# Gate applied where the heads' outputs leave PSUM, and a last norm summed on the tensor engine, in a two-layer hybrid trunk

## The chip, the core and the metric

The kernel runs on one core of a Trainium2 chip. The metric is the device time of one execution in microseconds (us). A core has engines that each run their own instructions in order: TensorE (PE; its weight loads are listed apart as PEld), VectorE (DVE), ScalarE (ACT), GpSimd (POOL) and SyncE (SP, which here only issues DMA transfers). SBUF is the on-chip memory that all engines read and write, PSUM the memory that PE writes its sums to, DRAM the large memory outside, reached by DMA.

## The reference

x is 1024 tokens of 1024 channels. Layer 1 mixes tokens with a diagonal state-space model (S5), layer 2 with a chunked gated DeltaNet of 12 heads of 128 channels; both add a 4-head cross attention into 256 memory tokens. What matters here is how layer 2 ends:

```python
h = rmsnorm(x, norm_w[i])
qkv, a, b, gate_mix, q_x, gate_x = jnp.split(h @ gdn_w_in[j], [...], axis=-1)
o = gated_delta_chunked(q, k, v, g, beta)            # 12 heads of 128
y_mix = rmsnorm(o, norm_w) * silu(gate_mix)          # 1536 channels
y_x = cross_attn(q_x, mem_h, w_mem_kv[i]) * silu(gate_x)    # 512 channels
x = x + concatenate([y_mix, y_x]) @ w_out[i]
return rmsnorm(x, final_norm_w)
```

## The kernel before

Everything is float32. A large product is made of three PE matmuls (`mm3`, L107): each operand is split into a high part, rounded to a short mantissa, and the rest (`split`, L84: the high part is a cast on ACT, L86, the rest a subtraction on DVE, L73). Weights come through a ring of two tiles each (`weight`, L114): `wraw` by DMA on ACT's queue, `whi` cast on ACT, `wlo` subtracted on DVE. Small helpers record most instructions, so their lines recur: `dma` L70 (SP's queue), `tt` L73, `ts` L77 and L79, `stt` L82, `mm` L48 and `transpose` L51 for PE. A tile scheduler, not the code's lines, sets the order on each engine, from the program's order and priorities; the engines keep to it. PSUM has four buffers `pp` for the large products and four `ps_a` for the rest.

Layer 2's DeltaNet runs over 8 chunks of 128 tokens, in two units of 6 heads each: `g_step` makes a unit's outputs `o` (with the products `r`, `vd`, `vn` and the state `S`), `g_norm` (L1242) normalises them, turns them with PE transposes into channels by tokens in `ps_a`, copies them on ACT with the norm's weight `gnw` into `oT` (L1264), and writes `oT` to DRAM (`oTd`). The gates, silu already applied, lie in DRAM as 12 tiles of 128 channels by 1024 tokens (`gate2`). `attention` makes one head's output `po` for 512 tokens, multiplies it by its gate tile `sg` into `yx` and writes `yx` to DRAM (`yT`, `yT2`).

The output projection of layer 2 runs in two halves of 512 tokens; the first half holds the tokens of chunks 0 to 3, the second those of 4 to 7. `out2_inputs(half)` makes the 16 input tiles of a half: four from the attention, then 12 from the heads. For a head's tile it loads `zr` from `oTd` and `zg` from the gate, multiplies them on POOL, and splits the product into `oh` and `ol`. `zr` and `zg` have three buffers in the first half and five in the second. `out2` then makes 8 output columns; each takes two weight tiles and 16 input tiles, adds the residual `xr` into `xo` and its squares, `sq`, to the sum `facc`. The first half's tiles are made beside the last attention heads and chunk steps (about 1648 to 1698 us), its columns beside the steps and norms of the last chunks (1698 to 1798), and the second half's tiles beside the first half's last columns (1798 to 1836).

The last column (`last_column`) is cut into two blocks of 256 tokens, so that the first block's norm runs beside the second block's products. The norm sums the 128 channels on PE into token columns (`rstd_cols`), takes the inverse root by three iterations on DVE (`rsqrt`, with names ending in e, t and h, and a sign turned at the end by a multiplication by −1), spreads it over the partitions with PE (`on_partitions`) and scales 8 columns (`out_scale`): columns 2 and 5 by ACT and POOL, the other six by one DVE instruction each.

Of the kernel before, what the change touches and what calls it, by code (L numbers as in the profile page):

```python
# [11 lines left out]
F32 = mybir.dt.float32  # L12
F32R = mybir.dt.float32r
I32 = mybir.dt.int32
AF = mybir.ActivationFunctionType
ALU = mybir.AluOpType
# [37 lines left out]
class Kern:  # L54
# [135 lines left out]
        self.ts(var, ss[:, 0:nt], 1.0 / nch, MUL, EPS, ADD)  # L190
        return self.rsqrt(wp, var, (128, nt), name)

    def on_partitions(self, wp, cols, name):

        out = []
        nt = cols.shape[1]
        for t0 in range(0, nt, 4):
            n = min(4, nt - t0)
            rb = self.pa.tile([128, 512], F32, name="ps_a", tag="ps_a")
            for t in range(n):  # L200
                dg = self.tl(wp, (128, 128), name + "dg", bufs=2)
                self.ts(dg, self.ident, cols[:, t0 + t:t0 + t + 1], MUL)
                self.pe.matmul(rb[:, 128 * t:128 * t + 128], lhsT=self.ones, rhs=dg, start=True, stop=True)
            out.append(rb[:, 0:128 * n])
        return out

    def rows_to(self, dst, halves):
        o = 0
# [71 lines left out]
    def attention(self, layer, h, half, ap, dst):  # L280
        scale = 128 ** -0.5
        hs = slice(512 * half, 512 * half + 512)
        kv = []
        for o in (0, 4):
            raw = self.tl(ap, (128, 256), f"kvr{o}")
            self.dma(raw, self.kvd[layer][o + h])
            kv.append([self.tl(ap, (128, 256), f"kv{o}{i}", F32R) for i in "hl"])
            self.split(raw, *kv[-1])
        (kh, kl), (vh, vl) = kv
        q, sg = self.tl(ap, (128, 512), "q"), self.tl(ap, (128, 512), "sg")  # L290
        self.dma(q, self.qx[h][:, hs])
        self.dma(sg, self.gx[h][:, hs])
        qh, ql = self.tl(ap, (128, 512), "qh", F32R), self.tl(ap, (128, 512), "ql", F32R)
        self.split(q, qh, ql)
        pr = self.tl(ap, (128, 4, 256), "pr")
        mx, sm = self.tl(ap, (128, 4), "mx"), self.tl(ap, (128, 4), "sm")
        for t2 in range(2):
            sc = self.pa.tile([128, 2, 256], F32, name="ps_a", tag="ps_a")
            for j in range(2):
                t = 2 * t2 + j  # L300
                s = slice(128 * t, 128 * t + 128)
                self.mm3(sc[:, j], (qh[:, s], ql[:, s]), (kh, kl), True, True)
            m = mx[:, 2 * t2:2 * t2 + 2]
            self.v.tensor_reduce(out=m, in_=sc, axis=AX, op=ALU.max)
            self.ts(m, m, -scale, MUL)
            for j in range(2):
                t = 2 * t2 + j
                self.act.activation(pr[:, t], sc[:, j], AF.Exp, bias=mx[:, t:t + 1], scale=scale,
                                    accum_out=sm[:, t:t + 1])
        self.v.reciprocal(out=sm, in_=sm)  # L310
        for t in range(4):
            self.ts(pr[:, t], pr[:, t], sm[:, t:t + 1], MUL)
        yield
        ph, pl = self.tl(ap, (128, 2, 512), "ph", F32R), self.tl(ap, (128, 2, 512), "pl", F32R)
        for b in range(2):
            pt = self.pa.tile([128, 512], F32, name="ps_a", tag="ps_a")
            for t in range(4):
                self.pe.transpose(pt[:, 128 * t:128 * t + 128], pr[:, t, 128 * b:128 * b + 128], self.ident)
            self.act.copy(ph[:, b], pt)
            self.tt(pl[:, b], pt, ph[:, b].bitcast(F32), SUB)  # L320
        po = self.pa.tile([128, 512], F32, name="ps_a", tag="ps_a")
        for b in range(2):
            d = slice(128 * b, 128 * b + 128)
            self.mm3(po, (vh[:, d], vl[:, d]), (ph[:, b], pl[:, b]), b == 0, b == 1)
        yx = self.tl(ap, (128, 512), "yx")
        self.tt(yx, po, sg, MUL)
        self.dma(dst[:, hs], yx)
        yield


# [911 lines left out]
    def g_norm(self, c, hf, o, gp):  # L1242

        act, pe, tt, ts = self.act, self.pe, self.tt, self.ts
        cs = slice(128 * c, 128 * c + 128)
        ss = self.tl(gp, (128, 6), "oss")
        for h in range(6):
            sq = self.tl(gp, (128, 128), "osq")
            act.activation(sq, o[:, h], AF.Square, accum_out=ss[:, h:h + 1])
        rq = self.rq[:, c, 3 * hf:3 * hf + 3].unsqueeze(2).broadcast_to([128, 3, 2])  # L1250
        s2 = ss.rearrange("p (j e) -> p j e", e=2)
        tt(s2, s2, rq, MUL)
        tt(s2, s2, rq, MUL)
        ts(ss, ss, 1.0 / 128, MUL, EPS, ADD)
        y = self.rsqrt(gp, ss, (128, 6), "on")
        y2 = y.rearrange("p (j e) -> p j e", e=2)
        tt(y2, y2, rq, MUL)
        tt(o, o, y.unsqueeze(2).broadcast_to([128, 6, 128]), MUL)
        oT = self.tl(gp, (128, 6, 128), "oT")
        for h0, n in ((0, 4), (4, 2)):  # L1260
            ps = self.pa.tile([128, 4, 128], F32, name="ps_a", tag="ps_a")
            for h in range(n):
                pe.transpose(ps[:, h], o[:, h0 + h], self.ident)
            act.activation(oT[:, h0:h0 + n], ps[:, 0:n], AF.Copy, scale=self.gnw)  # L1264
        self.dma(self.oT[6 * hf:6 * hf + 6, :, cs].rearrange("t p k -> p t k"), oT)


    def out2_inputs(self, half, yp, *pools):
        hs = slice(512 * half, 512 * half + 512)
        y = self.half_tiles(yp, 512, lambda i: 1)  # L1270
        for i, k in enumerate([12, 13, 14, 15] + list(range(12))):
            wp, n = pools[i % 5 // 3 if len(pools) > 1 else 0]
            t = self.tl(wp, (128, 512), "zr", bufs=n)
            if k >= 12:
                self.dma(t, self.yT2[k - 12, :, hs])
            else:
                g = self.tl(wp, (128, 512), "zg", bufs=n)
                self.dma(t, self.oT[k, :, hs])
                self.dma(g, self.gate2[k][:, hs])
                self.tt(t, t, g, MUL, self.pool)  # L1280
            self.split(t, y[i][0], y[i][1])
        return y

    def out2(self, half, y, wp):
        n = 512
        hs = slice(n * half, n * half + n)
        acc = self.tl(wp, (128, n), "facc")
        xo = []
        for ct in range(KD):
            w = self.A["w_out"][1, ct]  # L1290
            pieces = w[:, 0:8], w[:, 8:16]
            x = self.tl(wp, (128, n), "xr", bufs=2)
            k = slice(n // TAU * half, n // TAU * (half + 1))
            self.dma(x.rearrange("p (t k) -> p t k", t=TAU),
                     self.x1[ct].rearrange("p (t k) -> p t k", t=TAU)[:, :, k])
            xo.append(self.tl(wp, (128, n), f"xo{ct}"))

            def add(p, s):
                xs = x.rearrange("p (t k) -> p k t", t=TAU)[:, s.start // TAU:s.stop // TAU]
                self.tt(xo[ct][:, s].rearrange("p (k t) -> p k t", t=TAU), xs,  # L1300
                        p.rearrange("p (k t) -> p k t", t=TAU), ADD)
                self.square_sum(wp, acc[:, s], xo[ct][:, s], ct == 0)

            if half == 1 and ct == KD - 1:
                self.last_column(wp, pieces, y, add, xo, acc)
            else:
                add(self.project(pieces, y)[0], slice(0, n))
            yield
        if half == 0:
            s = slice(0, n)  # L1310
            rb, = self.on_partitions(wp, self.rstd_cols(wp, acc, 1024, "fn"), "fn")
            self.out_scale(wp, xo, rb, half, s)
            yield

    def last_column(self, wp, pieces, y, add, xo, acc):
# [14 lines left out]
        col = self.rstd_cols(wp, acc[:, blocks[0]], 1024, "fn")  # L1330
        products(1, 1)
        rb = self.on_partitions(wp, col, "fn")[0]
        add(ps[1], blocks[1])
        col = self.rstd_cols(wp, acc[:, blocks[1]], 1024, "fn")
        self.out_scale(wp, xo, rb, 1, blocks[0])
        self.out_scale(wp, xo, self.on_partitions(wp, col, "fn")[0], 1, blocks[1])

    def out_scale(self, wp, xo, rb, half, s):
        o = slice(512 * half + s.start, 512 * half + s.stop)
        n = s.stop - s.start  # L1340
        r = self.tl(wp, (128, n), "fr")
        self.act.copy(r, rb)
        for k in range(KD):
            if k % 3 == 2:
                self.act.activation(xo[k][:, s], xo[k][:, s], AF.Copy, scale=self.fnw[:, k:k + 1])
                self.tt(xo[k][:, s], xo[k][:, s], r, MUL, self.pool)
            else:
# [84 lines left out]
    def build(self):  # L1432
        tc = self.tc
        with ExitStack() as st:
# [6 lines left out]
            self.ud, self.gy = D("ud", 12, (TAU, 128, 128)), D("gy", 12, (TAU, 128, 128))  # L1441
            self.gate = D("gate", 12)
            self.yT = dr.tile([16, 128, L], F32, name="yT")
            self.x1, self.gate2 = D("x1", 8), D("gate2", 12)
            self.yT2 = dr.tile([4, 128, L], F32, name="yT2")
            self.qkvd = dr.tile([24, 128, L], F32, name="qkv")
            self.qkv = [self.qkvd[i] for i in range(24)]
# [94 lines left out]
```

## Time and profile before

| | us |
|---|---|
| median of 3 runs | 1940.75 |
| lowest and highest | 1936.44, 1943.25 |
| the profiled execution | 1942.68 |
| its span, first to last instruction | 1940.6 |

The profile is of one execution. Its lines name a line of the kernel, the engine, the operation, what it writes and reads (`out<-in`), shapes, counts, the busy time and the mean of one in ns, and the idle time of the engine before it with the work that ended it. The granted clock is that of PE, 1.0 being full speed; its mean over the span is 0.987. A line of a helper, L73 above all, stands for many places, so groups are told apart by the tiles' names.

### The profile page before, as it was taken

Reading aid. Unit: us, or ns where it says so; the run is one execution under the profiler, and the core shown is the slowest. Engines: PE = TensorE matmul, PEld = TensorE weight load, DVE = VectorE, ACT = ScalarE, POOL = GpSimd, SP = SyncE. Lnnn points to the kernel's source line nnn. Section 1 sums busy time; section 2 is a strip of 40 time slices with the busy share of each in tenths; the row PEclk is TensorE's granted clock in tenths of the full one; section 3 lists DMA queues with packets and bytes.
Section 4 is the critical chain, followed back from the end, with each engine's and each line's share of the span. In section 5 each row is a group of like instructions: output and inputs, shape, how many; then the busy total and the mean of one; then the engine's idle time right before and its main releaser. Section 6 shows DMA issues by size and latency. Waiting matters only on the chain.

```text
span 1940.6 us, 28754 instructions
## 1 busy us (share of the span) xinstructions
PE 1858.6 (96%) x10386; PEld 1527.3 (79%) x10386; DVE 1288.0 (66%) x2484; ACT 963.2 (50%) x2057; POOL 132.3 (7%) x87
## 2 busy tenths in 40 slices
PE   6899999999989998999999989999999999799897
PEld 6788888788878886888778878878777888688686
DVE  7888898896564422664556645888734876787644
ACT  5345688786454412443343456664434654555321
POOL 3000000000202231000000000000000000300400
PEclk9999999999999999999999999999999999999998
DMA  7445555655844343654312478776446656874752
GB/s 236 142 138 136 165 170 159 169 158 144 262 153 146 120 160 103 218 159 141 109 67 93 134 218 239 214 211 190 134 123 226 206 168 196 257 233 135 227 155 87
DMA packets 254397, 325.17 MB, mean 168 GB/s; under 512 B 80816, under 2 KB 176624, under 8 KB 254256
## 3 DMA queue, kind: packets, MB, share of 16 engines
q1 hardware_dynamic: 228912, 238.40, 39.7%
q10 hardware_dynamic: 25344, 84.95, 14.9%
q8 instruction: 82, 1.34, 0.3%
q14 instruction: 59, 0.48, 0.1%
HBM read 213.20 MB, written 93.95 MB: 158 GB/s over the span
## 4 chain that ended last, share of the span: by engine, by line
PE 75%; DVE 8%; DMA 8%; ACT 4%; issue 3%; SPq 1%; POOL 0%; DVEq 0%; ACTq 0%; POOLq 0%
PE pp L48 59%; PE ps_a L48 12%; PE ps_a L51 3%; DMA yr<-gy 2%; DVE wlo L73 1%; SPq L70 1%; DMA kv<-kvt 1%; DMA E<-Grow 1%; DMA zr<-yT 1%; DMA zr<-oTd 1%; DVE ol L73 0%; POOL zr L73 0%; ACT whi L86 0%; DMA kq<-qkv 0%; DMA x<-in_xT_dram 0%
## 5 line engine op out<-in xcount | busy, mean ns | idle before, releaser
L48 PE MATMUL pp<-hh,whi 128*128 128x512 f32 x1216 | 495.2, 408 | 0.0
L48 PE MATMUL pp<-hl,whi 128*128 128x512 f32 x1216 | 478.7, 394 | 3.7 <-DVE hl L82 3.7
L48 PE MATMUL pp<-hh,wlo 128*128 128x512 f32 x1216 | 478.0, 393 | 0.0
L86 ACT CAST whi<-wraw 128x1024 fp32r<-128x1024 f32 (+1 forms) x180 | 183.2, 1019 | 373.5 <-PE pp L48 351.8
L73 DVE TENSOR_TENSOR wlo<-wraw,whi 128x1024 fp32r<-128x1024 f32 (+2 forms) x180 | 218.0, 1211 | 101.5 <-ACT whi L86 100.9
L48 PEld LDWEIGHTS pp<-hh,whi 128*128 128x128 f32 x1216 | 229.7, 189 | 50.6 <-issue 5.3
L48 PEld LDWEIGHTS pp<-hh,wlo 128*128 128x128 f32 x1216 | 229.5, 189 | 48.4
L48 PEld LDWEIGHTS pp<-hl,whi 128*128 128x128 f32 x1216 | 229.8, 189 | 47.0 <-DVE hl L82 4.8
L48 PE MATMUL pp<-oh,whi 128*128 128x512 f32 (+1 forms) x528 | 208.3, 395 | 10.7 <-ACT oh L86 6.7
L48 PE MATMUL pp<-oh,wlo 128*128 128x512 f32 (+1 forms) x528 | 209.5, 397 | 3.0 <-DVE wlo L73 3.0
L48 PE MATMUL pp<-ol,whi 128*128 128x512 f32 (+1 forms) x528 | 208.8, 396 | 1.3 <-DVE ol L73 1.3
L48 PEld LDWEIGHTS pp<-oh,whi 128*128 128x128 f32 x528 | 100.6, 191 | 33.5 <-ACT oh L86 8.1
L48 PEld LDWEIGHTS pp<-ol,whi 128*128 128x128 f32 x528 | 100.7, 191 | 26.5 <-DVE ol L73 3.8
L48 PEld LDWEIGHTS pp<-oh,wlo 128*128 128x128 f32 x528 | 100.8, 191 | 24.7 <-DVE wlo L73 4.3
L48 PE MATMUL pp<-yl,whi 128*128 128x512 f32 x288 | 114.2, 396 | 0.5 <-DVE yl L73 0.5
L48 PE MATMUL pp<-yh,wlo 128*128 128x512 f32 x288 | 114.0, 396 | 0.0
L48 PE MATMUL pp<-yh,whi 128*128 128x512 f32 x288 | 113.5, 394 | 0.0
L73 DVE TENSOR_TENSOR pj<-pp,hr 128x512 f32<-128x512 f32 x104 | 69.0, 685 | 53.1 <-PE pp L48 53.1
L82 DVE SCALAR_TENSOR_TENSOR pj<-cx,conv_w,pj 128x1024 f32<-128x1024 f32 x72 | 92.3, 1282 | 1.4
L73 DVE TENSOR_TENSOR cx<-pp,hr 128x512 f32<-128x512 f32 x48 | 32.4, 689 | 91.0 <-PE pp L48 91.0
L73 POOL TENSOR_TENSOR ye<-yh,yl 128x1024 f32<-128x1024 f32 x12 | 29.7, 2475 | 620.3 <-DVE yl L73 444.9
L73 POOL TENSOR_TENSOR zr<-zr,zg 128x512 f32<-128x512 f32 x24 | 38.0, 1604 | 444.9 <-DMA kq<-qkv 308.9
(352 smaller groups left out, 3173.7 us busy)
## 6 DMA issues: line engine op xcount, KB each, us to landing
wraw<-in_w_out_dram ACTq DMA_DIRECT2D x64, 512.0 KB, 3.9
wraw<-in_g_w_in_dram ACTq DMA_DIRECT2D x44, 512.0 KB, 4.0
wraw<-in_s_w_in_dram ACTq DMA_DIRECT2D x32, 512.0 KB, 4.0
R<-E SPq DMA_DIRECT2D x48, 256.0 KB, 3.9
gate<-pj SPq DMA_DIRECT2D x24, 512.0 KB, 4.3
qkv<-pj SPq DMA_DIRECT2D x24, 512.0 KB, 2.6
kq<-qkv SPq DMA_DIRECT2D x60, 192.0 KB, 4.1
wraw<-in_w_glu_dram ACTq DMA_DIRECT2D x24, 384.0 KB, 3.6
```

Of the source, the lines that this page charges most:

```text
L48: return self.pin(self.eng.matmul(*a, **kw))
L51: return self.pin(self.eng.transpose(*a, **kw))
L70: self.nc.sync.dma_start(out=out, in_=in_)
L73: (eng or self.v).tensor_tensor(out=out, in0=a, in1=b, op=op)
L82: self.v.scalar_tensor_tensor(out=out, in0=a, scalar=s, in1=b, op0=op0, op1=op1)
L86: self.act.copy(hi, src)
```

## The change

1. `g_norm` of chunks 4 to 7 loads the unit's gate (`og`, 128 x 6 x 128, one buffer) and multiplies by norm weight and gate in one DVE instruction per PSUM tile, in place of ACT's copy. `gate2` becomes one DRAM tensor, so that one DMA reaches six heads.
2. `out2_inputs` of the second half loads no gate and multiplies nothing. In the first half the product moves from POOL to DVE.
3. `attention` multiplies in place into `sg`; the tile `yx` is gone.
4. The last block's norm (`negative_rstd`) adds `facc` and the last squares in PSUM, runs each iteration on single columns with one dependent step less, and leaves its result negative; the sign goes into `on_partitions`. It is recorded at high priority. In the first block of the last column, ACT and POOL scale columns 1, 3, 5 and 7 instead of 2 and 5.

```diff
-    def on_partitions(self, wp, cols, name):
+    def on_partitions(self, wp, cols, name, sign=None):
...
-                self.ts(dg, self.ident, cols[:, t0 + t:t0 + t + 1], MUL)
+                self.ts(dg, self.ident, cols[:, t0 + t:t0 + t + 1], MUL, sign, sign and MUL)
...
+    def negative_rstd(self, wp, parts, nch, name):
+        n = parts[0].shape[1] // 128
+        ss = self.pa.tile([128, 512], F32, name="ps_a", tag="ps_a")
+        for t in range(n):
+            for i, p in enumerate(parts):
+                self.pe.matmul(ss[:, t:t + 1], lhsT=p[:, 128 * t:128 * t + 128], rhs=self.ones[:, 0:1],
+                               start=i == 0, stop=i == len(parts) - 1)
+        x, h, t = (self.tl(wp, (128, n), name + c) for c in "vht")
+        e = self.tl(wp, (128, n), name + "e", I32)
+        y = e.bitcast(F32)
+        self.ts(x, ss[:, 0:n], 1.0 / nch, MUL, EPS, ADD)
+        self.ts(e, x.bitcast(I32), 1, ALU.logical_shift_right)
+        self.ts(h, x, 0.5, MUL)
+        self.ts(e, e, -1.0, MUL, 1597463007.0, ADD)
+        for _ in range(3):
+            for j in range(n):
+                c = slice(j, j + 1)
+                self.stt(t[:, c], y[:, c], y[:, c], h[:, c], MUL, MUL)
+            self.stt(y, t, 1.5, y, SUB, MUL)
+        return y
...
-        yx = self.tl(ap, (128, 512), "yx")
-        self.tt(yx, po, sg, MUL)
-        self.dma(dst[:, hs], yx)
+        self.tt(sg, po, sg, MUL)
+        self.dma(dst[:, hs], sg)
...
         oT = self.tl(gp, (128, 6, 128), "oT")
+        if c >= 4:
+            g = self.tl(gp, (128, 6, 128), "og", bufs=1)
+            self.dma(g, self.gate2[6 * hf:6 * hf + 6, :, cs].rearrange("t p k -> p t k"))
...
-            act.activation(oT[:, h0:h0 + n], ps[:, 0:n], AF.Copy, scale=self.gnw)
+            if c < 4:
+                act.activation(oT[:, h0:h0 + n], ps[:, 0:n], AF.Copy, scale=self.gnw)
+            else:
+                self.stt(oT[:, h0:h0 + n], ps[:, 0:n], self.gnw, g[:, h0:h0 + n], MUL, MUL)
...
+            elif half:
+                self.dma(t, self.oT[k, :, hs])
             else:
                 g = self.tl(wp, (128, 512), "zg", bufs=n)
                 self.dma(t, self.oT[k, :, hs])
                 self.dma(g, self.gate2[k][:, hs])
-                self.tt(t, t, g, MUL, self.pool)
+                self.tt(t, t, g, MUL)
...
-            def add(p, s):
+            def add(p, s, total=True):
...
-                self.square_sum(wp, acc[:, s], xo[ct][:, s], ct == 0)
+                if total:
+                    self.square_sum(wp, acc[:, s], xo[ct][:, s], ct == 0)
+                    return
+                sq = self.tl(wp, p.shape, "sq", bufs=2)
+                self.act.activation(sq, xo[ct][:, s], AF.Square)
+                return sq
...
-        add(ps[1], blocks[1])
-        col = self.rstd_cols(wp, acc[:, blocks[1]], 1024, "fn")
-        self.out_scale(wp, xo, rb, 1, blocks[0])
-        self.out_scale(wp, xo, self.on_partitions(wp, col, "fn")[0], 1, blocks[1])
+        sq = add(ps[1], blocks[1], False)
+        with self.tc.high_priority(offset=200):
+            col = self.negative_rstd(wp, (acc[:, blocks[1]], sq), 1024, "fz")
+            last = self.on_partitions(wp, col, "fn", -1.0)[0]
+        self.out_scale(wp, xo, rb, 1, blocks[0], (1, 3, 5, 7))
+        self.out_scale(wp, xo, last, 1, blocks[1])
...
-    def out_scale(self, wp, xo, rb, half, s):
+    def out_scale(self, wp, xo, rb, half, s, beside=(2, 5)):
...
-            if k % 3 == 2:
+            if k in beside:
...
-            self.x1, self.gate2 = D("x1", 8), D("gate2", 12)
+            self.x1 = D("x1", 8)
+            self.gate2 = dr.tile([12, 128, L], F32, name="gate2")
```

On DVE, where the first half's tiles are made (about 1670 us), before; a row is a line, an operation, what it writes and reads, and a shape, and `ol` is the rest of a tile's split:

```order
L73 TENSOR_TENSOR ol_15198<-zr,oh_15197 128x512
L77 TENSOR_SCALAR pr<-pr,sm 128x256 x4
L82 SCALAR_TENSOR_TENSOR r<-ps_a,nbr_9715,r 128x128 x2
L73 TENSOR_TENSOR ol_15200<-zr,oh_15199 128x512
L73 TENSOR_TENSOR ol_15202<-zr,oh_15201 128x512
L82 SCALAR_TENSOR_TENSOR r<-ps_a,nbr_9715,r 128x128 x3
L73 TENSOR_TENSOR vd<-ps_a,dlr_9716 128x512
```

The same place of the change:

```order
L73 TENSOR_TENSOR ol_15179<-zr,oh_15178 128x512
L73 TENSOR_TENSOR zr<-zr,zg 128x512
L77 TENSOR_SCALAR mx<-mx 128x2
L73 TENSOR_TENSOR r<-ps_a,gbe_8478 128x512
L73 TENSOR_TENSOR r<-ps_a,gbe_8478 128x256
L73 TENSOR_TENSOR ol_15181<-zr,oh_15180 128x512
L332 RECIPROCAL sm<-sm 128x4
L82 SCALAR_TENSOR_TENSOR r<-ps_a,nbr_9696,r 128x128
L73 TENSOR_TENSOR zr<-zr,zg 128x512 x2
```

The products `zr<-zr,zg` now stand on DVE between the chunk step's `r` and the attention's `mx`.

On ACT, where the second half's tiles are made (about 1798 to 1830 us), before; `oh` is the cast of a tile, `whi` that of a weight tile, and `whi_17043` and `whi_17081` belong to the last columns of the first half:

```order
L86 CAST oh3_16814<-zr_16852 128x512
L86 CAST whi_17043<-wraw_17042 128x1024
L86 CAST oh4_16816<-zr_16856 128x512
L86 CAST oh5_16818<-zr_16863 128x512
L86 CAST oh6_16820<-zr_16870 128x512
L123 DMA wraw_17110<-in_w_out_dram 128x1024
L86 CAST oh7_16822<-zr_16877 128x512
L86 CAST oh8_16824<-zr_16884 128x512
L179 ACTIVATE sq_17005<-xo5_16942 128x512
L86 CAST whi_17081<-wraw_17080 128x1024
```

The same place of the change:

```order
L86 CAST oh2_16801<-zr_16837 128x512
L86 CAST whi_17034<-wraw_17033 128x1024
L86 CAST oh3_16803<-zr_16841 128x512
L86 CAST oh4_16805<-zr_16845 128x512
L86 CAST oh5_16807<-zr_16849 128x512
L123 DMA wraw_17102<-in_w_out_dram 128x1024
L86 CAST oh6_16809<-zr_16853 128x512
L86 CAST oh7_16811<-zr_16857 128x512
L86 CAST whi_17064<-wraw_17063 128x1024
```

Five casts of tiles stand between two casts of weights in both; the weight casts now come one tile earlier, and the tiles wait for a load alone.

On SP's queue, where the last chunks' outputs are written (about 1760 to 1800 us), before:

```order
L70 DMA oTd<-oT 128x6x128
L70 DMA xr<-x_99 128x8x64
L70 DMA oTd<-oT 128x6x128
L70 DMA xr<-x_100 128x8x64
L70 DMA oTd<-oT 128x6x128 x2
L70 DMA zr<-yT_114 128x512
```

The same place of the change:

```order
L70 DMA oTd<-oT 128x6x128
L70 DMA og<-gate_102 128x6x128
L70 DMA oTd<-oT 128x6x128
L70 DMA og<-gate_102 128x6x128
L70 DMA xr<-x_100 128x8x64
L70 DMA oTd<-oT 128x6x128
L70 DMA og<-gate_102 128x6x128
L70 DMA oTd<-oT 128x6x128
L70 DMA xr<-x_101 128x8x64
L70 DMA zr<-yT_103 128x512
```

Each unit's gate load stands behind the write of the unit before, and `og` has one buffer.

## The prediction

> **What bounds the kernel now.** I read the page's busy times first, then the last 300 us by stage: in each row the stretch, its length, the busy time of PE, PEld, DVE, ACT and POOL (instructions in brackets), the granted clock, the DMA share and GB/s.
>
> ```profile
> PE 1858.6 (96%) x10386; PEld 1527.3 (79%) x10386; DVE 1288.0 (66%) x2484; ACT 963.2 (50%) x2057; POOL 132.3 (7%) x87
> ...
> 1648.00:1698.00 50.00, 40.28 (x200) 31.06 (x199) 40.00 (x95) 25.91 (x75) 17.51 (x12) 0.97 0.82 258
> 1698.00:1798.00 100.00, 99.37 (x562) 84.48 (x561) 80.51 (x253) 53.76 (x175) 0.00 (x0) 1.00 0.64 187
> 1798.00:1836.00 38.00, 30.96 (x124) 24.27 (x123) 30.92 (x27) 15.28 (x23) 20.48 (x12) 0.91 0.75 236
> 1836.00:1925.00 89.00, 89.00 (x437) 73.78 (x436) 38.33 (x67) 21.74 (x27) 2.55 (x2) 1.00 0.41 121
> 1925.00:1941.00 16.00, 3.22 (x18) 2.47 (x17) 9.02 (x34) 1.06 (x3) 3.00 (x4) 0.62 0.40 132
> ```
>
> PE is the bound with 96% of the span, and the change removes no product. So only PE's holes count, and the end, where PE has nothing left. Between 1698 and 1798 PE is full (99.37 of 100), and between 1836 and 1925 wholly so. The holes are 9.7 us in 1648–1698, where the first half's 16 tiles are made beside the chunk steps ("stage 1"), 7.0 us in 1798–1836, where the second half's are made ("stage 2"), and the tail from 1925. Apart from six instructions behind 1836, which belong to the final scaling, POOL works in these two stages alone: 12 gate products each, 1.46 us apiece in stage 1 and 1.71 in stage 2. The changed order of instructions departs from the old one only from about 1650 us on, apart from the gate loads of layer 1's attention, so the rest keeps its time.
>
> **Stage 2: the second half's tiles lose load and product.** The waits of PE, then of ACT, in 1800–1835 (us in total, times, longest), and the matmuls after PE's second stall (start, us):
>
> ```profile
> PE pp L48 <- ACT whi L86: 4.0, 1, 4.0
> PE pp L48 <- DVE wlo L73: 3.0, 2, 1.7
> ...
> ACT oh L86 <- POOL zr L73: 10.5, 9, 3.1
> ...
> 1819.62 0.63 PE L48 MATMUL pp<-oh,whi 128*128 128x512 f32 x1
> ...
> 1822.61 0.56 PE L48 MATMUL pp<-ol,whi 128*128 128x512 f32 x1
> ...
> 1823.23 0.40 PE L48 MATMUL pp<-oh,whi 128*128 128x512 f32 x1
> ...
> 1824.85 0.39 PE L48 MATMUL pp<-ol,whi 128*128 128x512 f32 x1
> ```
>
> PE waits for weights, not for tiles: `whi` is cast on ACT, and ACT runs its instructions in order; the casts of the second half's tiles stand ahead of `whi` and wait 10.5 us for POOL's products. So the products hold the weights of the last columns of the first half. PE then restarts slowly: seven steps of 0.43 us from 1819.62 to 1822.61, against 0.23 from 1823.23 to 1824.85 (seven again). Eight of them cost 8 x 0.20 = 1.6 us. Without the POOL products a tile needs a cast on ACT and a subtraction on DVE:
>
> ```profile
> L73 DVE TENSOR_TENSOR ol<-zr,oh 128x512 fp32r<-128x512 f32 x13 | 16.9, 1316 | 6.3 <-ACT oh L86 5.8
> ...
> L73 DVE TENSOR_TENSOR ol<-zr,oh x32: 676/692/1774, 1647.2 to 1830.7; 128x512 fp32r<-128x512 f32 x32
> ```
>
> The first row is stage 2 alone, the second all 32 (shortest, median, longest). Beside POOL the subtraction took 1.32 us; the shortest is 0.68. Twelve tiles at 0.69 are 8.3 us, where POOL needed 20.5. What can go is 7.0 + 1.6 = **8.6 us**. Late next is the tile chain itself: last transposes, write to DRAM, read, cast. The changed order puts about 9 us of PE's own products ahead of those last transposes, so less stands behind them to cover the chain; with the first casts waiting for the write, a short stall can stay. I take −8, with −8.6 and −4 (half of the stall left) as ends.
>
> **Stage 1: the product moves from POOL to DVE.** PE's largest waits in 1636–1700, the subtraction's row there, and two rows of the queue that issues the loads:
>
> ```profile
> PE ps_a L48 <- ACT ph L319: 2.9, 1, 2.9
> PE ps_a L48 <- ACT vn L1214: 2.8, 2, 2.1
> ...
> PE pp L48 <- ACT oh L86: 1.3, 1, 1.3
> PE pp L48 <- DVE ol L73: 1.3, 3, 0.7
> ...
> L73 DVE TENSOR_TENSOR ol<-zr,oh 128x512 fp32r<-128x512 f32 x16 | 13.2, 842 | 9.0 <-ACT oh L86 8.8
> ...
> 1656.70 0.33 SPq L70 DMA_DIRECT2D zg<-gate  x1
> 1657.14 2.50 SPq L70 DMA_DIRECT2D zr<-oTd  x3
> ```
>
> Only 2.6 us of the 9.7 are waits for tiles; `ph` and `vn` belong to the attention and the chunk steps, which share ACT and DVE with the tiles. A 128x512 product with both inputs in SBUF and no POOL beside it is priced by the subtraction, 0.69; 12 of them add 8.3 us to DVE, busy 40.0 of 50, and the subtractions give back 16 x (0.842 − 0.692) = 2.4. Net 5.9 of 10 us free. A tile's own chain shortens by 1.46 − 0.69 = 0.8 us; with three buffers the 12 pass in four turns, so the last tile comes 4 x 0.8 = 3 us earlier, and since the gate load at 1656.70 had to wait for a product and held the three loads behind it, perhaps 1.6 more. Against it: a product on DVE that waits for its load now holds what stands behind it on DVE, `r`, `vd` and the attention's `mx`, for which PE waits. If every tile wait and the lag they cause go, −8 (all but 1.7 of the holes); if the steps are held by one load in each turn (1 us, four turns), +4. I take **−3**, since the tiles' own waits are the row nearest to it.
>
> **The middle: the gate on DVE as the heads leave PSUM.** Eight units copy 128x512 and 128x256 with the gate. That form, PSUM and SBUF in, a scalar per partition, is the final scaling's:
>
> ```profile
> L82 DVE SCALAR_TENSOR_TENSOR xo<-xo,fnw,ps_a 128x256 f32<-128x256 f32 x12 | 5.3, 475 | 2.1 <-ACT fr L1342 2.1
> ...
> L82 DVE SCALAR_TENSOR_TENSOR xo<-xo,fnw,ps_a 128x512 f32<-128x512 f32 x6 | 4.3, 744 | 1.2 <-ACT fr L1342 1.2
> ```
>
> 8 x (0.744 + 0.475) = 9.8 us more on DVE, 19.5 of 100 being free, and as many copies fewer on ACT, which has 46 free. PE waited 0.6 there. Half the free DVE time goes, and the `vd`, `r` and state updates of the next step queue behind a unit's two copies (1.2 us). With one such delay in four of the eight uncovered it is +5; none, 0. I take **+2**. Twelve loads of 256 KB go and eight of 384 KB come: no traffic worth a term. Writing the attention's output into its gate tile makes the next gate load wait for the write:
>
> ```profile
> DMA to landing us min/median/max: 3.7/4.6/6.0
> ```
>
> That is the gate tile's own landing; the product that needs it stands a whole head later, so 0, at most +1.
>
> **The tail.** The last product is done when DVE adds the residual at 1925.75. DVE's chain to the end, with ACT's square and POOL's two products:
>
> ```profile
> 1925.75 0.60 DVE L73 TENSOR_TENSOR xo<-xr,pp 128x256 f32<-128x256 f32 x1
> 1927.23 0.66 DVE L73 TENSOR_TENSOR facc<-facc,sq 128x256 f32<-128x256 f32 x1
> 1928.58 0.16 DVE L79 TENSOR_SCALAR fnv<-ps_a 128x2 f32<-128x2 f32 x1 [0.30 <-PE ps_a L48]
> 1928.66 0.47 DVE L82 SCALAR_TENSOR_TENSOR xo<-xo,fnw,ps_a 128x256 f32<-128x256 f32 x1
> ...
> 1932.06 0.17 DVE L77 TENSOR_SCALAR fne<-fne 128x2 f32<-128x2 f32 x1
> 1932.27 0.48 DVE L77 TENSOR_SCALAR fndg<-ident,fne 128x128 f32<-128x128 f32 x2
> ...
> 1926.69 0.42 ACT L179 ACTIVATE sq<-xo 128x256 f32<-128x256 f32 x1
> ...
> 1926.88 1.59 POOL L73 TENSOR_TENSOR xo<-xo,fr 128x256 f32<-128x256 f32 x2 [61.68 <-ACT fr L1342]
> ```
>
> The sum's addition (0.66, with its handover about 0.8) goes to PE; the negation (1932.06 to 1932.27) takes 0.2; one dependent step of three less in each of three iterations saves about 0.1 each, since the two columns go one after the other; and two scalings fewer, 0.35 each, stand between the steps. 0.8 + 0.2 + 0.3 + 0.7 = 2.0. Against it stand four POOL products instead of two, 0.8 each, beside these steps. What POOL can do to small steps:
>
> ```profile
> 1680.71 3.05 POOL L73 TENSOR_TENSOR zr<-zr,zg 128x512 f32<-128x512 f32 x2 [0.68 <-DMA zr<-oTd]
> 1681.65 0.90 DVE L73 TENSOR_TENSOR oss<-oss,rq 128x6 f32<-128x6 f32 x1
> 1682.59 1.20 DVE L79 TENSOR_SCALAR oss<-oss 128x6 f32<-128x6 f32 x1
> ```
>
> Steps that take 0.16 alone took 0.90 and 1.20 there. I take **−1.5**, ends −2 and +0.5 (two steps held for a product each, 1.2 over).
>
> The Trainium skill ("SBUF — State Buffer", section "Who interferes with whom") says that a VectorE operation with two SBUF inputs contends with a GpSimd instruction that reads SBUF, and that a tensor_scalar in a two-port mode is shut out for the whole instruction. The rows at 1681.65 and 1682.59 agree, 0.90 and 1.20. By it the new iterations, all from SBUF, would stand in POOL's four products, and the tail would give 0 in place of −1.5.
>
> **The sum** against the profiled run, 1942.7 us with a span of 1940.6: −8 − 3 + 2 − 1.5 = −10.5, or 1932.2. That run lies 1.9 above the median of the runs, 1940.75, so against the median the time is **1930**.
>
> **Rivals.**
> - *POOL holds the tail*: the steps wait for the four products, the tail gives 0, all else as forecast: 1932. For it speak the held steps above; against, that only the part of the chain before about 1930 overlaps them.
> - *Stage 1 pays whole*, −8 in place of −3: 1925. For it speaks that `vn` and `ph` came late behind casts waiting for POOL; against, that DVE has only 10 us free there.
> - *DVE becomes the bound* between 1648 and 1798: stage 1 gives nothing, the middle costs +5: 1942.7 − 8 + 5 − 1.5 − 1.9 = 1936, no change. For it, 40.0 and 80.5 busy before anything is added.
> - *Slower: the single gate buffer.* A unit's gate load starts only after the unit before has been copied. The rows: the head outputs' last writes, and the landings of a load of the same shape (`vT`).
>
> ```profile
> 1774.14 0.36 SPq L70 DMA_DIRECT2D oTd<-oT  x1
> 1791.33 1.87 SPq L70 DMA_DIRECT2D oTd<-oT  x2
> ...
> DMA to landing us min/median/max: 3.3/4.2/8.3
> ```
>
> The last two units follow 1.5 us apart; load and copies in between take 4.2 + 1.2, at worst 8.3 + 1.2, so the last write comes 4 to 8 us later. It decides from where the last write is later than the first half's remaining products can cover; then stage 2 loses its gain and pays 8 + 1.6: 1942.7 − 3 + 2 − 1.5 + 9.6 − 1.9 = 1948. Against it: the write before those two lies 17 us earlier (1774.14), so one load of the two has time enough, and the products left after 1798 were held by weights, not by tiles.
>
> **How the numbers follow.** Forecast 0.48, tail held 0.12, stage 1 whole 0.13, DVE the bound 0.17, gate buffer 0.10. A measurement can tell about 0.3% (5.8 us) from no change: below 1934.9 is faster, above 1946.6 slower. The first three are faster save the forecast's upper edge (0.03): 0.70; the rest of it and DVE's case are within: 0.20; slower 0.10. The bounds of the forecast's terms and the neighbours give 1922 to 1940, which leaves out the gate buffer's case and the outermost of the others.
>
> **What would show it.** Right: PE's busy time in stage 2 near its length with the wait for `whi` gone and the clock at 1.0; ACT's waits for POOL gone in both stages; DVE at 85 to 90 of 100 in the middle with PE still over 97; `fnv` to `fndg` near 3 us instead of 3.7. Wrong: PE waiting in the middle for `vd`, `r` or `oT`; a wait of DVE's `oT` for the load of `og`; the second half's first casts waiting for the last write with PE empty; small steps of 0.5 us or more beside POOL in the tail.

## The result and the profile after

| | us |
|---|---|
| before, median of 17 runs | 1941.09 |
| the change, median of 17 runs | 1930.53 |
| ratio, with its 95% interval | 0.9945 (0.9932 to 0.9958) |
| the change's profiled execution | 1939.14 |
| its span | 1937.4 |

The change is faster by 10.6 us, by its interval 8.2 to 13.2. The profiled execution of the change is a long one, 8.6 us over its median, so the two spans can't be subtracted. Much of the excess lies ahead of the part that was changed. That is told by the tile view of `oh`, the high parts of the output projection's inputs, from 1640 us on; the columns are the count, the shortest, median and longest duration in ns, and the first and last start. Before:

```profile
L48 PE MATMUL pp<-oh,whi x272: 278/392/794, 1645.1 to 1925.2; 128*128 128x512 f32 x120, 128*128 128x256 f32 x16
```

and the change:

```profile
L48 PE MATMUL pp<-oh,whi x272: 278/392/628, 1651.2 to 1922.3; 128*128 128x512 f32 x120, 128*128 128x256 f32 x16
```

The first of these products starts 6.1 us later, after 1650 us of work that the change hardly touches: in the profiles of this study that start lies anywhere between 1640 and 1652. From the first to the last of them it is 280.1 us before and 271.1 after. This distance, called the **stretch** below, leaves the earlier parts out; what follows it is the tail.

Three windows, counted from the first product and called stage 1, the middle and stage 2 below, in the profile before (stretch of time, length, busy time of PE, PEld, DVE, ACT, POOL with counts, granted clock, DMA share, GB/s):

```profile
1645.10:1702.10 57.00, 46.61 (x232) 36.33 (x231) 46.63 (x117) 30.08 (x88) 17.51 (x12) 0.97 0.83 261
1702.10:1800.00 97.90, 97.27 (x550) 82.75 (x549) 78.45 (x242) 51.30 (x165) 0.00 (x0) 1.00 0.63 181
1800.00:1845.00 45.00, 37.96 (x154) 29.84 (x153) 30.52 (x25) 16.95 (x24) 20.48 (x12) 0.92 0.70 223
```

and of the change:

```profile
1651.20:1708.20 57.00, 48.82 (x233) 38.28 (x232) 45.97 (x119) 27.86 (x77) 0.00 (x0) 0.94 0.78 258
1708.20:1806.20 98.00, 95.80 (x546) 81.47 (x545) 86.06 (x263) 44.66 (x156) 0.00 (x0) 1.00 0.69 199
1806.20:1851.20 45.00, 44.93 (x198) 36.43 (x197) 25.67 (x32) 19.64 (x28) 0.00 (x0) 1.00 0.68 197
```

PE's idle time, the length less its busy time, goes from 10.4 to 8.2 us in stage 1, from 0.6 to 2.2 in the middle, and from 7.0 to 0.1 in stage 2, where the granted clock rises from 0.92 to 1.00. Idle time thus falls by 7.5 us of the 9.0 that the stretch loses. The rest is work that runs at another clock: a clock lower by 0.03 over the 57 us of stage 1 is worth some 1.7 us (an estimate from these rows), and stage 2 gains 0.08 over 45 us. So idle time has to be read together with the clock beside it. Two rows of the change, the first from its waits in 1651–1709 us, the second from the tile view of `zr`'s split:

```profile
PE ps_a L48 <- DVE r L73: 2.9, 1, 2.9
```

```profile
L73 DVE TENSOR_TENSOR ol<-zr,oh x32: 680/687/696, 1653.3 to 1832.9; 128x512 fp32r<-128x512 f32 x32
```

The wait for `whi` and `wlo` in stage 2 is gone. The subtraction, whose longest was 1.77 us beside POOL, takes 0.69 in all 32 places. New is a wait for `r`, a product of the chunk steps, which now stands on DVE behind the tiles' products. The chain of the change shows it: a load of `zr`, the product that waits for it, and `r` behind the product.

```profile
1675.96 6.93 DMA zr<-oTd
1682.99 0.69 DVE zr L73
1683.76 0.92 DVE r L73 x2
```

### The profile page after: what moved, and what is told of

Its sections match the earlier page's. It is cut to its first block, busy times and chain, and to the rows that moved or that the text cites. A ratio compares the mean times of both kernels' runs of the same rounds, so it can differ in the third digit from the quotient of the medians.

```text
span 1937.4 us, 28738 instructions
## 1 busy us (share of the span) xinstructions
PE 1865.1 (96%) x10390; PEld 1533.5 (79%) x10390; DVE 1284.0 (66%) x2508; ACT 958.1 (49%) x2043; POOL 95.8 (5%) x65
## 4 chain that ended last, share of the span: by engine, by line
PE 80%; DVE 7%; DMA 6%; ACT 4%; issue 2%; SPq 1%; DVEq 0%; ACTq 0%
PE pp L48 64%; PE ps_a L48 13%; PE ps_a L51 3%; DMA zr<-oTd 1%; SPq L70 1%; DVE wlo L73 1%; DMA yr<-gy 1%; ACT whi L86 0%; DVE pr L77 0%; DMA E<-Grow 0%; DVE ol L73 0%; ACT pr L330 0%; DMA XM<-Dm 0%; DMA R<-E 0%; DMA wraw<-in_s_w_in_dram 0%
## 5 line engine op out<-in xcount | busy, mean ns | idle before, releaser
L73 DVE TENSOR_TENSOR wlo<-wraw,whi 128x1024 fp32r<-128x1024 f32 (+2 forms) x180 | 212.9, 1183 | 94.4 <-ACT whi L86 93.2
L73 DVE TENSOR_TENSOR pj<-pp,hr 128x512 f32<-128x512 f32 x104 | 69.0, 686 | 54.8 <-PE pp L48 54.8
L73 DVE TENSOR_TENSOR cx<-pp,hr 128x512 f32<-128x512 f32 x48 | 32.5, 689 | 93.6 <-PE pp L48 93.6
L48 PEld LDWEIGHTS pp<-yl,whi 128*128 128x128 f32 x288 | 54.4, 189 | 12.4 <-DVE yl L73 0.8
L48 PEld LDWEIGHTS pp<-yh,wlo 128*128 128x128 f32 x288 | 54.4, 189 | 11.9
```

The source lines that it names most:

```text
L48: return self.pin(self.eng.matmul(*a, **kw))
L73: (eng or self.v).tensor_tensor(out=out, in0=a, in1=b, op=op)
```

## The experiments

Each run is one kernel with its own profile. Idle is PE's in the 57 us from the first product. Ratios are to runs of the kernel before on the same chip.

| run | what it is | stretch | idle | ratio (interval) |
|---|---|---|---|---|
| before | | 280.1 | 10.4 | |
| e3_tail_only | before, new tail | 281.8 | 9.8 | 1.0001 (0.9985 to 1.0017) |
| e2_half0_dve | before, first half's product on DVE | 279.8 | 8.3 | 0.9998 (0.9979 to 1.0016) |
| e6_half1_dve | before, second half's product on DVE | 274.8 | 10.5 | 0.9964 (0.9946 to 0.9982) |
| e1_fold_only | before, gate folded in for chunks 4 to 7 | 273.3 | 10.8 | 0.9954 (0.9937 to 0.9971) |
| e4_half0_pool | change, first half's product on POOL | 272.2 | 11.0 | 0.9958 (0.9940 to 0.9976) |
| r2_half0_pool_again | the same | 272.7 | 10.2 | 0.9948 (0.9929 to 0.9967) |
| the change | | 271.1 | 8.2 | 0.9945 (0.9932 to 0.9958) |
| r1_change_again | the change | 268.7 | 7.5 | 0.9938 (0.9916 to 0.9959) |
| t2_scale_after | the change up to the tail | 268.2 | 7.5 | 0.9943 (0.9923 to 0.9964) |
| t1_two_steps | the change up to the tail | 272.2 | 9.8 | one execution |
| t3_shared | every second product on POOL, tail of t2 | 270.9 | 8.8 | 0.9953 (0.9934 to 0.9971) |
| e10_half0_noprod | change without the first half's product | 267.8 | 6.5 | 0.9912 (0.9889 to 0.9935) |
| e11_half0_nogate | change without that product and its load | 267.9 | 5.9 | 0.9918 (0.9891 to 0.9946) |

One program's stretch varies: the four profiles of the change up to its tail give 268.2 to 272.2, the two of the kernel before 280.1 and 281.8, the three with the fold and POOL in the first half 272.2 to 273.3. So means of such groups are compared, and a single difference under some 3 us shows nothing by itself.

**The fold alone.**

```diff
+        if c >= 4:
+            g = self.tl(gp, (128, 6, 128), "og", bufs=1)
...
+                self.stt(oT[:, h0:h0 + n], ps[:, 0:n], self.gnw, g[:, h0:h0 + n], MUL, MUL)
...
+            elif half:
+                self.dma(t, self.oT[k, :, hs])
...
-        yx = self.tl(ap, (128, 512), "yx")
```

> The gate folded in for chunks 4 to 7 and none in the second half's tiles; the first half's product stays on GpSimd and the tail stays as before (the attention's output is written in place, to make room for the gate tile). The stretch is from the first to the last product of the output projection of layer 2: 280.1 us before, 271.1 with the whole change. Theory: this part alone carries the gain, the waits for whi in stage 2 are gone, stretch 270 to 273, time 8 to 10 us below before. Rival, that the first half's product on VectorE carries a third of it: stretch 274 or more, time 6 us below or less.

The stretch is 273.3, 0.3 outside the theory's range and short of the rival's 274; the ratio, 0.9954 or 8.9 us, is the theory's. With e4 and r2 the group's mean is 272.7 against 281.0 for the two profiles of the kernel before: the fold brings **8.3 us** net of what it costs in the middle.

**The first half's product alone, on DVE.**

```diff
-                self.tt(t, t, g, MUL, self.pool)
+                self.tt(t, t, g, MUL, self.pool if half else None)
```

> Only the first half's gate product moves from GpSimd to VectorE. Theory, that the loads into three buffers set the pace of the first half's tiles and not the product: stretch 279 to 281.5, time within 2 us of before. Rival (the forecast's term): stretch 277, time 3 us below before.

Stretch and time agree with the theory, and yet its reason was wrong for the gate's loads, as e10 and e11 show. The three windows of this run tell where the gain went:

```profile
1643.90:1700.90 57.00, 48.69 (x230) 37.90 (x230) 45.64 (x118) 28.16 (x78) 0.00 (x0) 0.94 0.86 278
1700.90:1798.90 98.00, 95.64 (x547) 81.13 (x546) 79.75 (x249) 51.59 (x172) 0.00 (x0) 1.00 0.60 168
1798.90:1843.90 45.00, 39.80 (x162) 31.38 (x161) 32.96 (x29) 19.20 (x27) 20.42 (x12) 0.92 0.75 233
```

PE's idle time in stage 1 falls by 2.1 us, from 10.4 to 8.3, but the granted clock there is 0.94 in place of 0.97, which by the estimate above costs some 1.7: PE ran 230 instructions in these 57 us, before 232. In the middle it is idle 2.4 us in place of 0.6, in stage 2 5.2 in place of 7.0. That adds up to about the 0.3 us of the stretch. In time, the interval reaches from 4.1 us below before to 3.1 above, so a gain of some 3 us is not excluded.

**The tail alone.**

```diff
-        col = self.rstd_cols(wp, acc[:, blocks[1]], 1024, "fn")
-        self.out_scale(wp, xo, rb, 1, blocks[0])
...
+            col = self.negative_rstd(wp, (acc[:, blocks[1]], sq), 1024, "fz")
...
+        self.out_scale(wp, xo, rb, 1, blocks[0], (1, 3, 5, 7))
```

> Only the last norm and the sharing of the first block's scaling change. Theory, from the profile of the change: from the last residual addition to the second block's first scaling 8.2 us in place of 8.6, no more, since the two single-column steps take as long as the two dependent ones; time within 1 us of before. Rival (the forecast's term): 7.1 us, time 1.5 us below.

It is 8.23 us, and no time that can be measured: the theory holds.

**The change with the first half's product back on POOL.**

```diff
-                self.tt(t, t, g, MUL)
+                self.tt(t, t, g, MUL, self.pool)
```

> The whole change, but the first half's product is put back on GpSimd. Theory, that this part gives nothing: stretch 270 to 272.5, time within 2 us of the change (9 to 11 us below before). Rival: stretch 274, time 3 us above the change.

The stretch, 272.2, is within the theory's range, while the time, 8.2 us below before, misses its 9 to 11. Both lie within the spread of single runs and settle nothing alone; r2 repeats the run.

**The second half's product on DVE, nothing folded.**

```diff
-                self.tt(t, t, g, MUL, self.pool)
+                self.tt(t, t, g, MUL, None if half else self.pool)
```

> The kernel before, but the second half's gate product moves from GpSimd to VectorE; its loads stay and nothing is folded in. Theory, that GpSimd's pace held the casts of the weights on ScalarE: PE's waits for whi and wlo between 1800 and 1840 fall from 7.0 us to under 2, stretch 272 to 275 (before 280.1). Rival, that the write to DRAM and the loads behind it set the pace: waits 5 us or more, stretch 278 or more.

PE's waits in 1800–1840 us, in total, times and longest:

```profile
PE pp L48 <- DVE wlo L73: 2.5, 3, 1.2
PE pp L48 <- ACT whi L86: 0.9, 1, 0.9
```

The 7.0 us became 3.4, not under 2, while the stretch, 274.8, is in the theory's range. The wait for `whi` fell from 4.0 to 0.9 as soon as POOL no longer set the pace, loads and writes being the same; what is left is `wlo`, made on DVE, where the products now stand too. So 6.2 us of the stretch (281.0 − 274.8, from one profile) come with the products leaving POOL. That not having them at all gives the remaining 2.1 of the 8.3 is not shown: it lies within the spread.

**The first half without its product, and without its load.**

```diff
                 g = self.tl(wp, (128, 512), "zg", bufs=n)
                 self.dma(t, self.oT[k, :, hs])
                 self.dma(g, self.gate2[k][:, hs])
-                self.tt(t, t, g, MUL)
```

> The change, with the first half's gate loaded but not multiplied (the product is left out). Theory, that the landings of the loads into three buffers set the pace of these tiles: stretch within 1.5 us of the change's 271.1. Rival, that the product's place and time on VectorE hold the chunk steps and the tiles: stretch 268.5 or less.

e11 leaves out the four lines but for the load of `zr`.

> The change, with neither load nor product of the first half's gate (12 loads of 256 KB and 12 products left out). Theory, that the loads set the pace: stretch 266 to 269, at least 2 us below the run that leaves out the product alone. Rival, that neither bounds and PE waits for the attention and the chunk steps: within 1 us of that run.

The first 57 us of the two, as windows:

```profile
1641.20:1698.20 57.00, 50.51 (x250) 40.73 (x249) 44.90 (x125) 29.85 (x87) 0.00 (x0) 0.94 0.86 274
```

```profile
1640.30:1697.30 57.00, 51.07 (x266) 41.84 (x264) 46.98 (x129) 31.66 (x90) 0.00 (x0) 0.97 0.75 231
```

Without the 12 loads the traffic falls from 274 to 231 GB/s, and the stretch does not move: 267.8 and 267.9. **The gate's 12 loads do not set the pace; that theory falls.** The loads of `zr` stay in both runs, and one of them stands in the change's chain above, so whether those set the pace was not tried. Both stretches lie 2.2 us below the mean of the change's four profiles, 270.05: so much, by these few, the product still costs on DVE. PE's wait for the `r` of L73, 1.4 to 2.9 us in those four, is in neither. In time the two are further off: 0.9912 and 0.9918 against 0.9938 to 0.9945 for the change, some 5 us. With four and five executions and overlapping intervals, what the stretch doesn't show of that stays open.

**The change and its POOL variant on one chip.** Both are repetitions.

> The change once more, on one chip with the next two. Theory, now that leaving out the product and the loads fell short of showing the loads as the pace: the product on VectorE instead of GpSimd is worth about 3 us of stretch, 268 to 271 here against 272 to 273.5 in the next run, and 2 to 3 us of time. Rival (my expectation of the earlier runs): stretches within 1 us of each other, times the same.

> The change with the first half's product on GpSimd, once more. Theory: stretch 272 to 273.5, PE idle in the 57 us from the first product some 2.5 us more than in the change, time 2 to 3 us above the change. Rival: no difference.

Their first 57 us, r1 and then r2:

```profile
1643.40:1700.40 57.00, 49.55 (x243) 38.62 (x243) 47.88 (x122) 28.72 (x79) 0.00 (x0) 0.97 0.82 267
```

```profile
1643.10:1700.10 57.00, 46.80 (x230) 37.47 (x230) 46.17 (x113) 29.43 (x86) 16.85 (x12) 0.94 0.82 258
```

Idle 7.5 against 10.2, stretch 268.7 against 272.7, medians 1930.62 and 1933.80: as the new theory has it. Some 1.7 of the 4.0 us go with the clock, 0.97 against 0.94. In the other pair, the change and e4, the clocks are the other way round, 0.94 and 0.97, and the stretches only 1.1 apart. The intervals of the two ratios overlap, so in time alone the 3 us are not shown; what speaks for them is that idle times, stretches and ratios of both pairs point one way.

**Two dependent steps for two single-column ones.**

```diff
-            for j in range(n):
-                c = slice(j, j + 1)
-                self.stt(t[:, c], y[:, c], y[:, c], h[:, c], MUL, MUL)
+            self.tt(t, y, y, MUL)
+            self.tt(t, t, h, MUL)
```

> The change, but each iteration of the last norm does its first part in two dependent steps on both columns, as before, in place of two single-column steps. Theory, that two single-column instructions take as long as two dependent ones: from the last residual addition to the second block's first scaling 8.2 us as in the change (within 0.15). Rival (the forecast's step): 8.5 us or more. Up to there it is the change again, so its stretch is a further look: 268 to 271.

It is 8.25 us, as the theory has it. One iteration of this run on DVE, and the start of the next:

```profile
1929.30 0.15 DVE L73 TENSOR_TENSOR fzt<-fze 128x2 f32<-128x2 f32 x1
1929.48 0.16 DVE L73 TENSOR_TENSOR fzt<-fzt,fzh 128x2 f32<-128x2 f32 x1
1929.68 0.16 DVE L82 SCALAR_TENSOR_TENSOR fze<-fzt,fze 128x2 f32<-128x2 f32 x1
1929.87 0.16 DVE L73 TENSOR_TENSOR fzt<-fze 128x2 f32<-128x2 f32 x1
```

The iteration takes 0.57 us; with single columns it takes 0.57 too (1927.36 to 1927.93 in the change, below). The stretch, 272.2, missed the 268 to 271 that the theory gave, and widened the spread told above.

**The first block's scalings behind the steps.** The DVE instructions from the last norm on are kept in the order of the program, where those scalings follow (`pinned` makes the helpers do so).

```diff
+        self.pinned = True
         with self.tc.high_priority(offset=200):
```

> The change, with the four VectorE scalings of the first block put behind the last norm's steps instead of between them. Theory, that three of them stand in the chain at some 0.27 us each: from the last residual addition to the second block's first scaling 7.4 to 7.6 us in place of 8.2, the four fitting the 1.6 us in which VectorE waits for the spread norm. Rival, that GpSimd's four products hold the bare steps: 8.0 us or more. In time under 1 us below the change.

```profile
1919.11 0.60 DVE L77 TENSOR_TENSOR xo<-xr,pp 128x256 f32<-128x256 f32 x1
...
1921.88 0.70 DVE L81 TENSOR_SCALAR fzh<-fzv 128x2 f32<-128x2 f32 x1
...
1922.68 0.69 DVE L86 SCALAR_TENSOR_TENSOR fzt<-fze,fzh 128x1 f32<-128x1 f32 x2
...
1925.16 4.10 DVE L86 SCALAR_TENSOR_TENSOR xo<-xo,fnw,ps_a 128x256 f32<-128x256 f32 x10
```

From the residual's addition to the end of the last scaling it is 10.15 us (1919.11 to 1929.26), where the change has 10.68: 0.53 won, a little less than the theory's 0.6 to 0.8. (The last scaling's end is taken because the row joins the ten scalings.) The steps, now bare, ran into POOL's four products (1920.45 to 1923.23): 0.70 in place of 0.16 and 0.69 in place of 0.35, so the rival's cost is there too. In time, 0.9943 against 0.9945, it can't be told from the change.

**Sharing the first half's products.** Those of odd tiles go to POOL, with the tail of t2.

```diff
-                self.tt(t, t, g, MUL)
+                self.tt(t, t, g, MUL, self.pool if k % 2 else None)
```

> The change with the four scalings of the first block behind the last norm's steps, and the first half's products shared, every second one on GpSimd. If the products on VectorE hold the chunk steps' r: stretch below the change, 267 to 269. If beside GpSimd the tiles and the small steps get slower as before: 270 to 273.

The stretch, 270.9, fits its second case, and the ratio is no better than the change's. No version that keeps the product beats the change clearly.

## Why the prediction was right

**Stage 2, forecast −8 (−8.6 to −4).** Idle time fell by 6.9 and the slow restart went with it. The mechanism is the one named: e6 takes the products off POOL and leaves everything else, and the wait for `whi` falls from 4.0 to 0.9 us. The short stall that was allowed for did not come: the casts waited for the loads of `zr`, 8.5 us in the change, with PE full.

**The middle, forecast +2 (0 to +5).** PE's idle time rose by 1.6 (0.6 to 2.2), but not by the path that the forecast names. PE did not wait for `vd`, `r` or the state behind a unit's copies; its one large wait there is for `one`, the small steps of a head's norm. The change, then e2:

```profile
PE ps_a L51 <- DVE one L82: 1.6, 1, 1.6
...
PE ps_a L51 <- DVE one L82: 1.2, 1, 1.2
```

e2 folds nothing in and is idle 2.4 us in the middle, so the rise is not shown to be the fold's. On DVE the folded copy cost what the final scaling's rows said: the tile view of `og` in the change has the 16 copies, eight of each width, and the load's landing.

```profile
L82 DVE SCALAR_TENSOR_TENSOR oT<-ps_a,gnw,og x16: 474/610/751, 1708.5 to 1807.1; 128x512 f32<-128x512 f32 x8, 128x256 f32<-128x256 f32 x8
...
DMA to landing us min/median/max: 4.0/4.7/6.5
```

The ends, 0.47 and 0.75 us, are the 0.475 and 0.744 of the forecast. Stage 2 and the middle together gave −8.3 in the runs, against −6 in the sum.

**Stage 1, forecast −3 (−8 to +4).** By the runs −2.7 (272.7 − 270.05), with the idle times of six profiles with POOL (9.8 to 11.0) and five with DVE (7.5 to 9.8) on the same side. It shows only with the fold; alone (e2) no gain can be told, for the clock and the middle took back what idle time gave. The counter-term of the forecast, that a product waiting for its load on DVE holds `r`, came in every profile with all the products on DVE: PE waits for it once behind the first product, 2.9 us in the change, 1.9 in r1, 1.4 in t2, 2.7 in t1 and 2.4 in e2. What went in exchange is the wait for `vn`, 1.5 to 2.8 us with POOL. The tiles' own waits, from which the −3 was taken, were 2.6 us before and still 1.1 to 2.7 in the four profiles of the change. So two terms that are not in the −3, `vn` and `r`, nearly cancel, and that the size came out so near is partly luck.

**The tail, forecast −1.5 (−2 to +0.5): mis-sized.** The change, on DVE and then on POOL:

```profile
1922.91 0.60 DVE L73 TENSOR_TENSOR xo<-xr,pp 128x256 f32<-128x256 f32 x1
...
1925.41 0.16 DVE L79 TENSOR_SCALAR fzv<-ps_a 128x2 f32<-128x2 f32 x1 [0.72 <-PE ps_a L48]
1925.49 0.47 DVE L82 SCALAR_TENSOR_TENSOR xo<-xo,fnw,ps_a 128x256 f32<-128x256 f32 x1
1925.88 0.49 DVE L77 TENSOR_SCALAR fze<-fzv 128x2 int32<-128x2 int32 x1
...
1926.74 0.31 DVE L79 TENSOR_SCALAR fze<-fze 128x2 int32<-128x2 int32 x1
...
1927.36 0.34 DVE L82 SCALAR_TENSOR_TENSOR fzt<-fze,fzh 128x1 f32<-128x1 f32 x2
1927.73 0.16 DVE L82 SCALAR_TENSOR_TENSOR fze<-fzt,fze 128x2 f32<-128x2 f32 x1
1927.93 0.35 DVE L82 SCALAR_TENSOR_TENSOR fzt<-fze,fzh 128x1 f32<-128x1 f32 x2
...
1929.09 0.48 DVE L79 TENSOR_SCALAR fndg<-ident,fze 128x128 f32<-128x128 f32 x2
1931.15 2.44 DVE L82 SCALAR_TENSOR_TENSOR xo<-xo,fnw,ps_a 128x256 f32<-128x256 f32 x6 [1.58 <-ACT fr L1379]
...
1924.26 2.77 POOL L73 TENSOR_TENSOR xo<-xo,fr 128x256 f32<-128x256 f32 x4 [61.89 <-ACT fr L1379]
```

From the residual's addition to the second block's first scaling it is 8.24 us, before 8.58 (1925.75 to 1934.33): −0.34, and 8.23 to 8.25 in e3, e4, r1, r2 and t1. What failed is the forecast's 2.0 us of savings. The sum of squares on PE brought 0.33 of the 0.8: `fzv` starts 2.50 after the addition, before 2.83. From there to `fndg` it is 3.68, before 3.69, where the prediction looked for 3: the iterations got no shorter (t1), the negation's 0.2 and a scaling fewer between the steps are eaten by POOL, under whose products two steps of 0.16 took 0.49 and 0.31. Taking POOL's four products as equal, an estimate from their row, the third ends at 1926.34 and the fourth at 1927.03; the two held steps end at 1926.37 and 1927.05. So the rival in which POOL holds the tail (0) was nearer than the forecast's −1.5. The Trainium skill's rule that was cited for it ("SBUF — State Buffer", section "Who interferes with whom") is borne out by these two rows, and the two of t2.

**The sum.** −8.3 − 2.7 − 0.3 = −11.3, against −10.6 measured (8.2 to 13.2) and a forecast of −10.5: the tail's 1.2 us too many and the 2.3 too few of stage 2 and the middle partly cancel, so that the total came this close is luck in part. That the attention's output is written in place was not tried apart, since it makes room for the gate tile; a cost of 1 us would be lost in the spread of the first product's start.

**The other rivals.** Stage 1 did not pay whole, −2.7 of the −8. DVE did not become the bound: 86 of 98 us in the middle with PE at 95.8. The single gate buffer came near its limit and was covered: in the change the last load, issued at 1802.00, was used from 1806.45 on. A wait of DVE's `oT` for a load of `og`, which the prediction named as a sign of being wrong, did come in other runs, once in each: 2.0 us in r1, 1.4 to 1.6 in t2, e1, e4 and r2. PE did not wait for it: in stage 2 of these runs it was busy through all 45 us.

## What to carry to other kernels

An engine that is slow and little used can still set the pace of the busiest one, where a third engine takes its results in order with that one's weights: look at what is queued behind a wait, not at the share of busy time. Of many instructions moved, the few that stood in such a queue brought the gain; the same move, product for product, gave about 6 us in one stage and 3 or less in another. Idle time alone does not tell what such a move is worth: the clock beside it does, and so do the waits that come in its place. The chain of tiny dependent steps was not shortened by splitting them into single columns, and such a chain should not run beside the products of an engine that holds it, as POOL's held these.

## What the runs showed of the hardware

Two single-column instructions that don't depend on each other take 0.34 to 0.35 us on DVE, as long as two dependent ones on both columns, though two independent steps on both columns start 0.08 apart in the same profile of the change:

```profile
1920.12 0.17 DVE L77 TENSOR_SCALAR fne<-fnv 128x2 int32<-128x2 int32 x1
1920.20 0.16 DVE L77 TENSOR_SCALAR fnh<-fnv 128x2 f32<-128x2 f32 x1
```

What makes the single columns wait was not tried. And one program gave a stretch of 268.2 to 272.2 us in four executions, not all on the same chip, the two long ones with a longest wait of PE in stage 1 of 2.9 us (2.2 and 2.3 in the others), and a granted clock of 0.94 there in place of 0.97. By that clock alone they would differ by some 1.7 us of 57 (an estimate from these figures).
